# A hybrid decoder step: its last stage in scaled fp16 parts instead of fp32r parts, with weights split once

## The chip, the cores and the metric

The kernel runs on one core of a Trainium2 chip. The metric is the device time of one execution in microseconds (us). The core's engines run side by side: TensorE (PE in the profile; its weight loads are listed apart as PEld), VectorE (DVE), ScalarE (ACT), GpSimd (POOL), and SyncE (SP), which here issues nearly all DMAs, in its program's order. Every engine takes its own instructions in order and waits for the others by semaphores.

## The reference, cut to what matters

2048 prompt rows and 64 sample rows of width 1024 go through one mixer layer. All branches read the same normalised, conditioned `h`:

```python
proj = h @ w_in                                   # 1024 -> 10240
u_a, v_a, z_a, q, k, v, z_b, gate_logits = jnp.split(proj, SPLIT_IDX, axis=-1)
y_a = u_a * zs.reshape(bsz, s, A_WIDTH) * jax.nn.silu(z_a)      # zs: spatial gating of the normalised v_a
y_b = attn.reshape(bsz, s, B_OUT).astype(x.dtype) * jax.nn.silu(z_b)
g_a, g_b = jnp.split(jax.nn.sigmoid(gate_logits), 2, axis=-1)
merged = g_a * (y_a @ w_proj_a) + g_b * (y_b @ w_proj_b)        # 1024 -> 1024 and 512 -> 1024
out = merged @ w_out                                            # 1024 -> 1024
x_new = x + gate[:, None, :] * _rmsnorm(out, g_post)
```

All of it is float32 in the reference. The change touches the last four lines, and the place of some work that surrounds them.

## The kernel before

Each matrix product is done in parts: an operand is split into a high part H and a rest L, and three matmuls (H·H, L·H, H·L) add up in PSUM (`mm_cm`, lines 391 to 399, channels on partitions; `mm_tm`, lines 401 to 409, rows on partitions). For `w_in` the parts are fp16, scaled by a measured maximum (`parts`, lines 323 to 359: ACT takes the absolute maximum, then H on ACT at line 349 and L on DVE at line 350). In the last stage the parts are fp32r, without a scale.

The stages that matter here follow one another so:

1. Attention, with the q, k, v, z_b products and units 0 to 12 of the 16 gate units (`gates`, each 128 of the 2048 gate columns) woven in. Rows of `y_b` go to the DRAM tensor `yb_d` (`y_rows`, lines 1007 to 1013).
2. The four `v_a` units (lines 1118 to 1133), whose rows go to DRAM (`va_d`) and whose statistics are kept; then gate units 13 and 14 (lines 1134 to 1137).
3. Gating (lines 1192 to 1222): for each of 8 channel groups, `gating(g)` reads `va_d` back into tiles `vg`, ACT normalises them (line 1175), PE multiplies them with the spatial weights (line 1176) and DVE makes `zs` of that; the u and z units of the group follow in 5 column groups, with SiLU, and the product is written to `ya_d` (line 1213). `gating(g+1)` is woven into the matmuls of group g, but `gating(0)` stands alone ahead of them.
4. The first block of `y_a` is split (`y_split`, line 1247), under gate unit 15 (line 1248).
5. The last stage (lines 1262 to 1328): four blocks of rows, 512, 512, 512 and 576. Per block `y_a` and `y_b` are loaded and split, then for 8 groups of 128 channels PE makes the two projections (24 and 12 matmuls), DVE and ACT merge them with the gates and split the result (`mH`, `mL`, lines 1291 to 1295), and then the output product runs for 4 groups of 256 columns over the 4 or 5 row tiles of the block (line 1304, 24 matmuls each). `load_unit` (lines 293 to 305) loads and splits all three weights anew in every block. After the last column group of a row tile, the row tile of `x` is loaded into `xt`, the normalised product is added in place, and `xt` is written out (lines 1314 to 1328); `xt` has 3 buffers.

The order on each engine is set by a scheduler, which lists the instructions by times that it works out itself; `late` (lines 76 to 86) keeps one from being placed far ahead of its neighbours. Tiles of one tag take turns in a ring of `bufs` buffers, and a load into one waits for the last reader of the tile that was there. PSUM banks are rings too: three of tag `mm`, one each of `s0`, `s1` and `o`, two of `t` (line 100).

Of the kernel before, what the change touches and what calls it, by code (L numbers as in the profile page):

```python
# [69 lines left out]
def body(ctx, tc, I, O):  # L70
# [222 lines left out]
    def load_unit(w, c0, nc_=256, nkc=KC):  # L293

        out = []
        kt = 512 // nc_
        for j in range(0, nkc, kt):
            raw = wt.tile([128, kt, nc_], F32, tag="wr", bufs=6, name="wr")
            DMA(raw, w[j * 128:(j + kt) * 128, c0:c0 + nc_].rearrange("(k p) c -> p k c", p=128))
            H = wt.tile([128, kt, nc_], F32R, tag="wh", bufs=7, name="wh")  # L300
            L = wt.tile([128, kt, nc_], F32R, tag="wl", bufs=7, name="wl")
            S.activation(H, raw, AF.Copy)  # L302
            (nc.gpsimd if j == 4 else V).tensor_tensor(L, raw, H, op=ALU.subtract)  # L303
            out += [(H[:, k, :], L[:, k, :]) for k in range(kt)]
        return out

# [126 lines left out]
    def sample_attention(sp):  # L433
# [75 lines left out]
        for hp in range(4):  # L509
# [624 lines left out]
    for c in (13, 14):  # L1134
# [61 lines left out]
    for g in range(8):  # L1196
# [4 lines left out]
        for j, (t0, n) in enumerate(groups):  # L1201
# [32 lines left out]
    wt = fx.enter_context(tc.tile_pool(name="wt", bufs=1))
    f2 = None

    def y_split(pool, nm, src, k, c0, n):
        raw = (f2.tile([128, 576], F32, tag="raw", bufs=3, name="raw") if c0 else
               wt.tile([128, 512], F32, tag="wr", bufs=6, name="raw"))
# [117 lines left out]
```

## Time and profile before

| what | before |
|---|---|
| time, median of 3 runs | 2597.12 us (2596.55 to 2605.16) |
| time of the profiled execution | 2591.6 us |
| its span, first to last instruction | 2589.8 us |
| mean granted TensorE clock | 0.984 |
| PE busy | 2476.3 us, 96% of the span |
| DVE, ACT, POOL busy | 1610.8, 1123.6, 337.7 us |

The span is divided by time: attention and its products up to about 1640 us, the gating stage from 1706 to 2086 us, the last stage from 2110 to 2590 us. A matmul is pipelined, so its duration in the profile is longer than the time that it adds to a stream; that time is the distance between two starts, called the pitch here. Idle time of an engine that is not the bottleneck costs nothing.

### The profile page before, as it was taken

How to read it: one execution, taken by the hardware profiler on the slowest of the kernel's cores; microseconds unless marked ns; L12 is line 12 of the kernel's file. 1: busy time of each engine (PE TensorE's matmuls, PEld its weight loads, DVE VectorE, ACT ScalarE, POOL GpSimd, SP SyncE). 2: the span in 40 equal slices, each digit the busy share in tenths (PEclk: the TensorE clock that was granted, in tenths of full speed). 3: DMA queues.
4: the chain of work that ended last, by engine and by line, in shares of the span. 5: the costliest groups of instructions: out<-in, count | busy, mean ns of one | idle time of the engine just before them, and what ended most of it. 6: DMA issues, size and time to landing. Idle time of an engine off the chain costs nothing.

```text
span 2589.8 us, 48446 instructions
## 1 busy us (share of the span) xinstructions
PE 2476.3 (96%) x18518; PEld 1771.1 (68%) x18518; DVE 1610.8 (62%) x3630; ACT 1123.6 (43%) x2791; POOL 337.7 (13%) x458
## 2 busy tenths in 40 slices
PE   6899999989989999899899999999999999999998
PEld 3775867857668555555455688756565568898998
DVE  5743446788868788677796885665333245555653
ACT  5644565455545545444454432332232234343422
POOL 0210000220121211212113121011000011111110
PEclk7999999999999999999999999999999999999999
DMA  6323644666875777857768774352212066656552
GB/s 247 111 77 67 171 110 116 141 172 164 195 170 125 172 162 184 168 128 172 160 171 206 184 208 151 94 177 85 72 59 63 26 208 212 203 169 216 187 161 73
DMA packets 529992, 384.22 MB, mean 148 GB/s; under 512 B 185087, under 2 KB 472975, under 8 KB 529758
## 3 DMA queue, kind: packets, MB, share of 16 engines
q1 hardware_dynamic: 505150, 315.48, 45.1%
q0 software_dynamic: 24608, 65.63, 9.4%
q8 instruction: 145, 2.38, 0.4%
q14 instruction: 89, 0.73, 0.1%
HBM read 250.85 MB, written 90.78 MB: 132 GB/s over the span
## 4 chain that ended last, share of the span: by engine, by line
PE 58%; DMA 13%; DVE 12%; issue 11%; ACT 3%; POOL 1%; SPq 0%; DVEq 0%; ACTq 0%; POOLq 0%
PE mm L397 12%; PE mm L398 12%; PE mm L399 12%; DMA ch<-in_cache_kv_w 5%; PE mm L407 3%; PE mm L408 3%; PE mm L409 3%; DVE S L527 2%; DVE pr L526 1%; PE s L407 1%; PE s L1176 1%; PE s L409 1%; PE s L408 1%; PE o L409 1%; PE o L408 1%
## 5 line engine op out<-in xcount | busy, mean ns | idle before, releaser
L397 PE MATMUL mm<-hH,hl 128*128 128x512 f16 (+2 forms) x2240 | 767.6, 343 | 0.4 <-DVE xsm L428 0.4
L398 PE MATMUL mm<-hL,hl 128*128 128x512 f16 (+2 forms) x2240 | 767.0, 342 | 0.0
L399 PE MATMUL mm<-hH,hl 128*128 128x512 f16 (+2 forms) x2240 | 766.9, 342 | 0.0
L407 PE MATMUL mm<-hl,hH 128*128 128x256 f16 x1536 | 416.9, 275 | 13.7 <-ACT vt L676 10.9
L408 PE MATMUL mm<-hl,hL 128*128 128x256 f16 x1536 | 420.0, 275 | 3.7 <-DVE hL L668 3.4
L409 PE MATMUL mm<-hl,hH 128*128 128x256 f16 x1536 | 419.7, 274 | 0.5 <-DVE hl L350 0.5
L397 PEld LDWEIGHTS <-hl 128*128 128x128 f16 x2240 | 222.3, 99 | 182.9 <-issue 9.6
L399 PEld LDWEIGHTS <-hl 128*128 128x128 f16 x2240 | 219.6, 98 | 180.1 <-DVE hl L350 0.4
L398 PEld LDWEIGHTS <-hl 128*128 128x128 f16 x2240 | 219.9, 98 | 170.3 <-issue 1.0
L925 ACT ACTIVATE p<-p,sg 128x256 f32<-128x256 f32 (+1 forms) x384 | 172.4, 450 | 160.0 <-DVE sg L923 144.3
L454 POOL DMA_DIRECT2D ch<-in_cache_kv_w x104 | 93.1, 896 | 719.4 <-DVE pr L588 203.5
L408 PEld LDWEIGHTS <-hL 128*128 128x128 f16 x1536 | 151.3, 99 | 37.4 <-issue 13.6
L407 PEld LDWEIGHTS <-hH 128*128 128x128 f16 x1536 | 151.9, 99 | 28.0 <-issue 6.9
L409 PEld LDWEIGHTS <-hH 128*128 128x128 f16 x1536 | 151.5, 99 | 18.6 <-issue 0.4
L303 POOL TENSOR_TENSOR wl<-wr,wh 128x512 fp32r<-128x512 f32 x48 | 63.4, 1321 | 693.2 <-ACT wh L302 638.4
L302 ACT ACTIVATE wh<-wr 128x512 fp32r<-128x512 f32 x160 | 100.3, 631 | 120.3 <-PE mm L398 69.6
L923 DVE CUSTOM_DVE_ANT_0 p<-s,masks,cqk 128x256 f32<-128x256 f32 (+1 forms) x384 | 140.8, 419 | 14.6 <-PE s L915 14.3
L349 ACT ACTIVATE hl<-wr,scw 128x512 f16<-128x512 f32 x160 | 107.3, 713 | 82.0 <-DVE scw L341 77.3
L1209 ACT ACTIVATE e<-mm,scw 128x512 f32<-128x512 f32 (+2 forms) x40 | 24.5, 613 | 261.3 <-PE mm L399 261.3
L943 DVE SCALAR_TENSOR_TENSOR hl<-p,hl 128x1024 f16<-128x1024 f32 (+2 forms) x100 | 95.3, 954 | 51.3 <-ACT hl L942 50.8
L350 DVE SCALAR_TENSOR_TENSOR hl<-wr,scw,hl 128x512 f16<-128x512 f32 x160 | 114.9, 745 | 15.8 <-ACT hl L349 15.6
L397 PE MATMUL mm<-yaH,wh 128*128 128x512 f32 (+1 forms) x320 | 112.9, 353 | 0.5 <-DVE gts L1291 0.5
(441 smaller groups left out, 4619.2 us busy)
## 6 DMA issues: line engine op xcount, KB each, us to landing
ch<-in_cache_kv_w POOLq DMA_DIRECT2D x104, 512.0 KB, 6.0
wr<-in_w_in SPq DMA_DIRECT2D x160, 256.0 KB
wr<-in_w_proj_a SPq DMA_DIRECT2D x64, 256.0 KB
wr<-in_w_out SPq DMA_DIRECT2D x64, 256.0 KB
a<-sg SPq DMA_DIRECT2D x48, 264.0 KB
c<-a SPq DMA_DIRECT2D x48, 264.0 KB
v<-vt SPq DMA_DIRECT2D x96, 128.0 KB
vr<-v SPq DMA_DIRECT2D x48, 256.0 KB
```

The lines of the kernel that those rows point to most:

```text
L302: S.activation(H, raw, AF.Copy)
L349: S.activation(HL[:, 0], raw, AF.Copy, scale=sc[:, 0:1])
L350: V.scalar_tensor_tensor(HL[:, 1], raw, sc[:, 0:1], HL[:, 0], op0=ALU.mult, op1=ALU.subtract)
L397: PE.matmul(pt, h, xh[:, t0:t0 + n], start=kc == 0, stop=False)
L398: PE.matmul(pt, h, xl[:, t0:t0 + n], start=False, stop=False)
L399: PE.matmul(pt, l, xh[:, t0:t0 + n], start=False, stop=kc == m - 1)
L407: PE.matmul(pt, xh[:, t0:t0 + n], h, start=kc == 0, stop=False)
L408: PE.matmul(pt, xl[:, t0:t0 + n], h, start=False, stop=False)
L409: PE.matmul(pt, xh[:, t0:t0 + n], l, start=False, stop=kc == m - 1)
L923: V.tensor_tensor_reduce(x, sb[e][:, j, 0:nk], masks[:, 256 - nk:256], scale=cqk[:, i:i + 1], scalar=3e38, op0=ALU.add, op1=ALU.min, accum ...
L925: S.activation(x, x, AF.Exp, bias=mc, scale=-1.0, accum_out=lc)
L943: V.scalar_tensor_tensor(ll, x2, PSCALE, hh, op0=ALU.mult, op1=ALU.subtract)
```

## The change

- In the last stage both operands of all three products become scaled fp16 parts (`split`). Each scale is one over a global maximum: of each weight matrix (`wmx`, 40 tiles, scanned by 40 extra DMAs and 40 reductions on DVE during gating, `scan_weights`), and of `y_a` and `y_b` (`ymx`, one reduction for each piece written). The five maxima are brought together ahead of the last stage by a short chain over DVE, PE and DVE again (tiles `um`, `m1`, `fm`).
- The weights are loaded and split once (`weights16`) and stay on chip for all four blocks; the POOL's share of the splitting is gone. `w_proj_a`, the first block of `y_a` and `w_proj_b` are split under the last two gate units, `w_out` during the first block.
- Gate unit 14 is moved from between the `v_a` units and gating to the end of gating, next to unit 15.
- The merge takes one more ACT instruction per group (a scaled copy), the output product takes its PSUM banks from `s0`, `o`, `s1`, `t` in turn, and `xt` has 2 buffers instead of 3. The loads of `y_a` and `y_b` take a ring of 6 buffers (`raw`) which the weights share.

```diff
@@ plan
-        order.extend((OG + c * 128, 128) for c in (13, 14))
+        order.append((OG + 13 * 128, 128))
         for g in range(8):
             order.extend((o + g * 128, 128) for o in (OU, OZ))
-        order.append((OG + 15 * 128, 128))
+        order.extend((OG + c * 128, 128) for c in (14, 15))
@@ y_rows (and the same for the sample rows)
         S.activation(yT, pt, AF.Copy)
+        V.tensor_reduce(ymx[:, 40 + 5 * hp + q:41 + 5 * hp + q], yT, axis=AX.X, op=ALU.max, apply_absolute_value=True)
         DMA(yb_d[hp * 128:(hp + 1) * 128, q * 512:(q + 1) * 512], yT)
@@ after the v_a units
-    for c in (13, 14):
+    for c in (13,):
@@ gating stage
+    def scan_weights():
+        prev = None
+        for i, src in enumerate(tail_tiles()):
+            raw = wp.tile([128, 512], F32, tag="wr", bufs=WRB, name="wsc")
+            DMA(raw, src)
+            if prev is not None:
+                late(V.tensor_reduce(wmx[:, i - 1:i], prev, axis=AX.X, op=ALU.max, apply_absolute_value=True))
+            prev = raw
+            yield
...
             DMA(ya_d[g * 128:(g + 1) * 128, t0:t0 + n], zs[:, t0:t0 + n])
+            V.tensor_reduce(ymx[:, 5 * g + j:5 * g + j + 1], zs[:, t0:t0 + n], axis=AX.X, op=ALU.max,
+                            apply_absolute_value=True)
+            next(scan)
@@ between gating and the last stage
+    def split(pool, tag, raw, n, s, width=512):
+        H = pool.tile([128, width], F16, tag=tag + "H", bufs=1, name=tag + "H")
+        L = pool.tile([128, width], F16, tag=tag + "L", bufs=1, name=tag + "L")
+        S.activation(H[:, 0:n], raw[:, 0:n], AF.Copy, scale=s)
+        V.scalar_tensor_tensor(L[:, 0:n], raw[:, 0:n], s, H[:, 0:n], op0=ALU.mult, op1=ALU.subtract)
+        return H, L
+    um = f0.tile([128, 2, 5], F32, name="um")
+    for i, (x, lo, hi) in enumerate(((wmx, 0, 16), (wmx, 16, 24), (wmx, 24, 40), (ymx, 0, 40), (ymx, 40, 64))):
+        V.tensor_reduce(um[:, 0, i:i + 1], x[:, lo:hi], axis=AX.X, op=ALU.max)
+    pt = bank("t")
+    PE.transpose(pt[0:5, 0:128], um[:, 0, :], ident)
...
+    PE.matmul(pb[:, 0:5], ones[0:5, :], m1[:, 0:5], start=True, stop=True)
...
+    def weights16(pool, nm, w, nkc, s):
+        out = []
+        for k in range(nkc):
+            hl = []
+            for h in range(2):
+                raw = f0.tile([128, 576], F32, tag="raw", bufs=6, name="raw")
+                DMA(raw[:, 0:512], w[k * 128:(k + 1) * 128, h * 512:(h + 1) * 512])
+                hl.append(split(pool, f"{nm}{k}{h}", raw, 512, s))
+                yield
+            out.append(hl)
+        parts16[nm] = out
...
+    def first_block():
+        yield from weights16(f0, "wa", w_a, 8, um[:, 1, 0:1])
+        for k in range(8):
+            ya0.append(y_split(f0, "ya", ya_d, k, 0, 512, um[:, 1, 3:4]))
+            yield
+        yield from weights16(f0, "wb", w_b, 4, um[:, 1, 1:2])
-    ya0 = [y_split(f0, "ya", ya_d, k, 0, 512) for k in range(8)]
-    for _ in gates(15):
+    fb = first_block()
+    for c in (14, 15):
+        for _ in gates(c):
+            next(splitting)
+            for _ in range(3):
+                next(fb, None)
+    for _ in fb:
         pass
@@ last stage
-                    if k not in units:
-                        units[k] = [load_unit(w_a, k * 128, 128, 8), load_unit(w_b, k * 128, 128, 4)]
...
-                H = f1.tile([128, 576], F32R, tag=f"mH{c}", name=f"mH{c}")
+                H = f1.tile([128, 576], F16, tag=f"mH{c}", name=f"mH{c}")
...
+                    mm_cm(pa[:, 0:gn], unit_of("wa", c * 128, 128), ya, t0, gn)
...
+                    S.activation(ga, ga, AF.Copy, scale=fm[:, 0:1])
...
-                uo = load_unit(w_o, u * 256, 256, 8)
+                uo = unit_of("wo", u * 256, 256)
...
-                    po = bank(("s", "o")[i % 2])
+                    po = bank("sost"[i % 4])
...
-                    xt = f2.tile([128, D], F32, tag="xt", bufs=CXB, name="xt")
+                    xt = f2.tile([128, D], F32, tag="xt", bufs=2, name="xt")
```

The scheduler makes a new order of all this. Three places of it matter for what follows; rows of the changed kernel carry its own line numbers.

First, ScalarE at the start of gating, where `gt` is the eviction of a gate unit, `vg` the normalising of `gating(0)` and `hl` a weight split. Before:

```order
L720 ACTIVATE gt<-mm,scw 128x320
L349 ACTIVATE hl<-wr,scw 128x512 x2
L720 ACTIVATE gt<-mm,scw 128x512 x2
L1175 ACTIVATE vg<-vg,nb,rs 128x128 x2
L720 ACTIVATE gt<-mm,scw 128x512
L1175 ACTIVATE vg<-vg,nb,rs 128x128 x2
```

With the change:

```order
L711 ACTIVATE gt<-mm,scw 128x512 x2
L711 ACTIVATE gt<-mm,scw 128x256
L1167 ACTIVATE vg<-vg,nb,rs 128x128 x6
L711 ACTIVATE gt<-mm,scw 128x320
L1167 ACTIVATE vg<-vg,nb,rs 128x128
L339 ACTIVATE hl<-wr,scw 128x512
```

Before, the first `vg` stands behind all of unit 13 and two pieces of unit 14; now six `vg` stand ahead of the last piece of unit 13, and on PE the first matmul on `vg` follows 6 matmuls after unit 13.

Second, VectorE and PE at the end of gating, where the maxima come together (`um` the maxima by partition, `m` and `fm` what follows from them). VectorE with the change:

```order
L1224 SCALAR_TENSOR_TENSOR zs<-e,scw,zs 128x256
L1227 TENSOR_REDUCE ymx<-zs 128x1
L1217 SCALAR_TENSOR_TENSOR zs<-mm,scw,zs 128x320
L1223 SCALAR_TENSOR_TENSOR e<-e,mm 128x320
L1224 SCALAR_TENSOR_TENSOR zs<-e,scw,zs 128x320
L1227 TENSOR_REDUCE ymx<-zs 128x1
L1263 TENSOR_REDUCE um<-wmx 128x1 x3
L1263 TENSOR_REDUCE um<-ymx 128x1 x2
L1267 TENSOR_REDUCE m_24528<-t 5x1
L1268 TENSOR_SCALAR m_24528<-ident,m_24528 5x5
L1271 TENSOR_SCALAR um<-t 128x5
L1272 RECIPROCAL um<-um 128x5
```

and PE in the middle of gate unit 14:

```order
L388 MATMUL mm<-hL_112,hl 128x512
L1265 MATMUL t<-ident,um 5x128
L389 LDWEIGHTS hl
...
L389 MATMUL mm<-hH_109,hl 128x512
L1270 MATMUL t<-m_24528,ones 128x5
L387 LDWEIGHTS hl
```

The transpose of the maxima (line 1265) stands behind 38 matmuls of width 512 of unit 14, and the matmul that spreads them (line 1270) behind 22 more; no split of a weight can start earlier.

Third, SP at the very end. Before:

```order
L1328 DMA out<-xt 128x512 x2
L1316 DMA xt<-in_x_prompt 128x1024
L1328 DMA out<-xt 128x512 x4
L1316 DMA xt<-in_x_sample 64x1024
L1328 DMA out<-xt 128x512 x2
L1326 DMA out<-xt 64x512 x2
```

With the change:

```order
L1392 DMA out<-xt 128x512 x2
L1380 DMA xt<-in_x_prompt 128x1024
L1392 DMA out<-xt 128x512 x3
L1380 DMA xt<-in_x_prompt 128x1024
L1392 DMA out<-xt 128x512
L1380 DMA xt<-in_x_sample 64x1024
L1392 DMA out<-xt 128x512 x2
L1390 DMA out<-xt 64x512 x2
```

With two buffers three of the five loads of `xt` stand between writes, where two did.

More of the change, by code (lines that the diff above doesn't have):

```diff
@@ L161, in body @@
     vmx = const.tile([128, 3, 4, 16], F32, name="vmx")
+    wmx = const.tile([128, 40], F32, name="wmx")
+    ymx = const.tile([128, 64], F32, name="ymx")
+    V.memset(ymx, 0.0)
     w_cond = I["w_cond"][0]
+    w_a, w_b, w_o = I["w_proj_a"][0], I["w_proj_b"][0], I["w_out"][0]
     def x_src(i):
@@ L291, in gate_rows @@
             DMA(gg_d[:, n * 512:(n + 1) * 512], gr[:, 0, :])
[L293 to L305, printed above, removed]
     order, units, raws = [], {}, []
@@ L1190, in gating, with tail_tiles @@
         yield
+    def tail_tiles():
+        for w, n in ((w_a, 8), (w_b, 4), (w_o, 8)):
+            for k in range(n):
+                for h in range(2):
+                    yield w[k * 128:(k + 1) * 128, h * 512:(h + 1) * 512]
+    def scan_weights():
[7 more added lines that the diff above has]
+            yield
+        late(V.tensor_reduce(wmx[:, 39:40], prev, axis=AX.X, op=ALU.max, apply_absolute_value=True))
+        while True:
+            yield
+    scan = scan_weights()
     gen = gating(0)
@@ L1229, in body @@
     sx_.close()
+    next(scan)
     fx = ExitStack()
     f0 = fx.enter_context(tc.tile_pool(name="f0", bufs=1))
[L1234 to L1239, printed above, removed]
-        DMA(raw[:, 0:n], src[k * 128:(k + 1) * 128, c0:c0 + n])
-        H = pool.tile([128, 576], F32R, tag=f"{nm}H{k}", name=f"{nm}H{k}")
-        L = pool.tile([128, 576], F32R, tag=f"{nm}L{k}", name=f"{nm}L{k}")
-        S.activation(H[:, 0:n], raw[:, 0:n], AF.Copy)
-        V.tensor_tensor(L[:, 0:n], raw[:, 0:n], H[:, 0:n], op=ALU.subtract)
-        return H, L
@@ new lines, in body @@
+    pb = bank("t")
+    PE.matmul(pb[:, 0:5], ones[0:5, :], m1[:, 0:5], start=True, stop=True)
+    V.tensor_scalar(um[:, 0], pb[:, 0:5], 1.0 / 8192.0, 1e-30, op0=ALU.mult, op1=ALU.max)
+    V.reciprocal(um[:, 1], um[:, 0])
+    fm = f0.tile([128, 6], F32, name="fm")
+    for i in range(2):
+        V.tensor_tensor(fm[:, i:i + 1], um[:, 0, i:i + 1], um[:, 0, 3 + i:4 + i], op=ALU.mult)
+    V.scalar_tensor_tensor(fm[:, 2:3], fm[:, 1:2], 0.5, fm[:, 0:1], op0=ALU.mult, op1=ALU.add)
+    V.tensor_scalar(fm[:, 2:3], fm[:, 2:3], 2.0 ** 37 / 2.0 ** 15, 1e-30, op0=ALU.mult, op1=ALU.max)
@@ new lines, in unit_of, with y_split @@
+    def unit_of(nm, c0, nc_):
+        h, o = divmod(c0, 512)
+        return [(x[h][0][:, o:o + nc_], x[h][1][:, o:o + nc_]) for x in parts16[nm]]
+    parts16 = {}
+    def y_split(pool, nm, src, k, c0, n, s):
+        raw = f0.tile([128, 576], F32, tag="raw", bufs=6, name="raw")
+        DMA(raw[:, 0:n], src[k * 128:(k + 1) * 128, c0:c0 + n])
+        return split(pool, f"{nm}{k}", raw, n, s, 576)
+    def first_block():
+        yield from weights16(f0, "wa", w_a, 8, um[:, 1, 0:1])
+        for k in range(8):
+            ya0.append(y_split(f0, "ya", ya_d, k, 0, 512, um[:, 1, 3:4]))
+            yield
+        yield from weights16(f0, "wb", w_b, 4, um[:, 1, 1:2])
@@ L1263, in body @@
             mg = []
[L1264 to L1282 removed]
+            ya = [y_split(f0, "ya", ya_d, k, c0, n, um[:, 1, 3:4]) for k in range(8)] if c0 else ya0
+            yb = [y_split(f2, "yb", yb_d, k, c0, n, um[:, 1, 4:5]) for k in range(4)]
+            for c in range(8):
+                H = f1.tile([128, 576], F16, tag=f"mH{c}", name=f"mH{c}")
+                L = f1.tile([128, 576], F16, tag=f"mL{c}", name=f"mL{c}")
                 gt = f2.tile([128, 2, 576], F32, tag="gts", bufs=2, name="gts")
@@ L1296, in body @@
                 mg.append((H, L))
+                for _ in range(2):
+                    next(wo, None)
+            for _ in wo:
+                pass
             tl = [(t, min(128, n - t)) for t in range(0, n, 128)]
```

39 lines of the change are left out of this document (17 added, 22 removed).

## The prediction

> **What bounds the kernel now.** I read the page first, then the busy times by stretch of time, then the list of waits of PE in the last stage.
>
> ```profile
> span 2589.8 us, 48446 instructions
> PE 2476.3 (96%) x18518; PEld 1771.1 (68%) x18518; DVE 1610.8 (62%) x3630; ACT 1123.6 (43%) x2791; POOL 337.7 (13%) x458
> ```
>
> ```profile
> 1200.00:1400.00 200.00, 178.89 (x1365) 105.69 (x1363) 149.71 (x327) 91.61 (x240) 34.50 (x51) 0.96 0.73 174
> 1706.00:2086.00 380.00, 379.22 (x2234) 224.06 (x2233) 150.20 (x293) 108.93 (x250) 17.28 (x27) 1.00 0.22 70
> 2110.00:2582.00 472.00, 466.93 (x3073) 429.28 (x3072) 245.54 (x440) 177.42 (x390) 61.62 (x47) 1.00 0.57 182
> ```
>
> After the stretch each row gives PE, PEld, DVE, ACT and POOL busy, the granted clock, the DMA share and GB/s. Gating (second row) and the last stage (third) are PE's: it is idle for 0.8 and 5.1 us of them, at full clock. DVE has room there (150 of 380, 246 of 472 us), DMA too. In attention (first row) PE is idle for 21 of 200 us while DVE is busy for 150.
>
> ```profile
> PE s L407 <- DVE ot L1310: 3.6, 3, 1.6
> PE mm L397 <- DVE gts L1291: 0.5, 1, 0.5
> PE s L407 <- ACT mH L1294: 0.5, 1, 0.5
> ```
>
> So the splitting and reloading of weights in the last stage costs the end nothing now: PE waits for none of it. Removing 160 ACT splits, 160 DVE or POOL subtractions and some 20 MB of loads (two passes over 10.5 MB of weights instead of four) is worth nothing by itself. What can be won there is the pitch of PE's matmuls; what can be lost is cover at the seams.
>
> **Term 1, the pitch.** These are starts of matmuls in PE's order of time, the first and the last of a run without a gap: fp32r with `y_a` (24 matmuls), `y_b` (9), width 288 (17) and the output product (24); then fp16 of width 512, 256 and 320 (24 each).
>
> ```profile
> 2152.24 0.39 PE L397 MATMUL mm<-yaH,wh 128*128 128x512 f32 x1
> 2157.47 0.39 PE L399 MATMUL mm<-yaH,wl 128*128 128x512 f32 x1
> 2150.13 0.40 PE L397 MATMUL mm<-ybH,wh 128*128 128x512 f32 x1
> 2152.00 0.40 PE L399 MATMUL mm<-ybH,wl 128*128 128x512 f32 x1
> 2446.80 0.29 PE L399 MATMUL mm<-yaH,wl 128*128 128x288 f32 x1
> 2448.91 0.29 PE L397 MATMUL mm<-yaH,wh 128*128 128x288 f32 x1
> 2420.94 0.28 PE L407 MATMUL o<-wh,mH 128*128 128x256 f32 x1
> 2423.62 0.28 PE L409 MATMUL o<-wl,mH 128*128 128x256 f32 x1
> ```
>
> ```profile
> 1726.29 0.38 PE L398 MATMUL mm<-hL,hl 128*128 128x512 f16 x1
> 1731.26 0.38 PE L397 MATMUL mm<-hH,hl 128*128 128x512 f16 x1
> 1701.78 0.27 PE L397 MATMUL mm<-hH,hl 128*128 128x256 f16 x1
> 1704.29 0.27 PE L399 MATMUL mm<-hH,hl 128*128 128x256 f16 x1
> 1704.55 0.30 PE L397 MATMUL mm<-hH,hl 128*128 128x320 f16 x1
> 1707.67 0.30 PE L399 MATMUL mm<-hH,hl 128*128 128x320 f16 x1
> ```
>
> fp32r: 5.23/23 = 0.2274 us with `y_a`, 1.87/8 = 0.2338 with `y_b`, 2.11/16 = 0.1319 at 288, 2.68/23 = 0.1165 at 256. fp16: 4.97/23 = 0.2161 at 512, 2.51/23 = 0.1091 at 256, 3.12/23 = 0.1357 at 320. Width 288 in fp16 stands in no row; halfway between 256 and 320 it is 0.1224. The counts are from the code: three blocks of 512 give 3·8·24 = 576 matmuls with `y_a` and 288 with `y_b`; the fourth block runs 2·8·36 = 576 of width 288; the output product 4·17·24 = 1632 of width 256. So 576·0.0113 = 6.5, 288·0.0177 = 5.1, 576·0.0095 = 5.5, 1632·0.0074 = 12.1: **−29.2 us**. With the 288s at the pitch of 320 or of 256 it would be −21.5 or −36.9; the three fp16 rows lie on a line, so I keep −29.2 within 1.
>
> The Trainium skill, "TensorE: Matmul & The Clock Gate", section "Back-to-back issue gap", gives the warm gap as N/2.4 ns plus 2.5 ns and names no type. By that alone both kinds would run at 0.2158, 0.1225 and 0.1092 us and this term would be zero. The trace agrees with it for fp16 and not for fp32r, so the rows decide.
>
> **Term 2, `gating(0)` loses half of its cover.**
>
> ```profile
> 1664.75 0.38 ACT L427 ACTIVATE xsm<-mm 64x256 f32<-64x256 f32 x1 [0.66 <-PE mm L417]
> 1686.54 1.48 SPq L1169 DMA_DIRECT2D vg<-va  x3
> 1689.85 6.25 DMA vg<-va
> 2171.49 2.88 DMA raw<-ya
> 1710.51 0.49 PE L1176 MATMUL s<-wT,vg 128*128 128x128 f32 x2 [0.78 <-ACT vg L1175]
> 1710.77 5.49 ACT L1175 ACTIVATE vg<-vg,nb,rs 128x128 f32<-128x128 f32 x14
> ```
>
> The first row is the end of the `v_a` units on PE (1664.7), and the two gate units behind it end at about 1707.8, so one takes 21.5 us. The loads of `vg` are issued from 1686.5, held back by the statistics and the `lr` tiles, not by PE, and the small last one lands at 1696.1. Before, unit 14 covered that; PE waited 0.8 us. Now PE has unit 13 only, to 1686.2, and 6 matmuls (1.3 us): it asks for `vg` at 1687.5. The first quarter can land between 2.9 us after its issue (a read of `ya_d` of the same size, the third row from below) and 6.25 us: 1689.4 to 1692.8; one normalising later PE has stood for 2.3 to 5.7 us. From there 16 normalisings at 0.39 us (5.49/14) take as long as the 16 small and some 20 wide matmuls between them, but an eviction and a split (0.5 and 0.7 us) stand in ACT's line. **+5 us**, bounds +2 and +9.
>
> **Term 3, the start of the last stage.** Unit 14 now helps here: two units, 43 us, cover the maxima and 32 tiles, then the first projection (24·0.2161 = 5.2 us) covers 4 tiles of `y_b`.
>
> ```profile
> 2088.74 0.53 ACT L1209 ACTIVATE e<-mm,scw 128x320 f32<-128x320 f32 x1 [6.05 <-PE mm L399]
> 2089.82 0.55 DVE L1211 SCALAR_TENSOR_TENSOR zs<-e,scw,zs 128x320 f32<-128x320 f32 x1
> 2110.00:2130.00 20.00, 19.49 (x85) 15.66 (x85) 8.47 (x13) 7.03 (x13) 3.57 (x3) 1.00 0.87 270
> 2185.68 0.69 DVE ybL L1244
> ```
>
> ```profile
> L349 ACT ACTIVATE hl<-wr,scw 128x512 f16<-128x512 f32 x160 | 107.3, 713 | 82.0 <-DVE scw L341 77.3
> L350 DVE SCALAR_TENSOR_TENSOR hl<-wr,scw,hl 128x512 f16<-128x512 f32 x160 | 114.9, 745 | 15.8 <-ACT hl L349 15.6
> ```
>
> Let T be the end of the last z matmul (2088.5 in this trace). The last `zs` is done at T+1.9, its maximum and the five small ones at about T+3. But PE's order puts the transpose behind 38 matmuls, T+8.2, and the spreading behind 60, T+13.0; with the small DVE steps the first split starts at about T+14. The six tiles of the ring have landed by then, and DVE takes them at 0.745 us each: T+19. From there each tile needs its load. At the 270 GB/s of the third row 262 KB take 0.97 us. Until the first tile of `y_b` that is 27 tiles, and about 1.2 MB of gate results to write, worth 4.7 more: 31.7·0.97 = 31 us, T+50. PE asks at T+42.8+5.2 = T+48, and the other three `y_b` tiles come 0.97 us apart against 0.65 us of matmuls each: **+3 us**. ACT needs 24·0.713+4 us of gate evictions for the tiles of the first projection, so it is not the bound. If a tile took as long as at a block's seam (from that read at 2171.49 to the last row of the first fence: 12 tiles with a ring of 3 in 14.9 us, 1.24 each, or 1.65 if three had been loaded before), it would be +11 to +23; if DVE alone set the pace, 0.745, nothing. Bounds 0 and +12.
>
> **Term 4, the end.** `xt` has two buffers.
>
> ```profile
> 2570.89 0.42 DVE L1310 SCALAR_TENSOR_TENSOR ot<-s,ggp 128x256 f32<-128x256 f32 x1 [2.39 <-ACT sq L1309]
> 2575.72 0.34 SPq L1316 DMA_DIRECT2D xt<-in_x_prompt  x1
> 2576.62 4.57 DMA out<-xt
> 2581.21 3.83 DMA xt<-in_x_sample
> ```
>
> The chain that ends last is not PE there, but the ring: a write of 4.57 us, a load of 3.83. Call the first row (row tile 0 of the last columns) E. The load that waits for tile 0's write is issued at E+4.8 (second row), the sample rows land at E+14.2, and the span ends at E+18.9. With two buffers tile 2 loads at E+4.8 and lands near E+8.7; tile 3 waits for tile 1's write, loads near E+10 and lands near E+13.8; the sample tile waits for tile 2's write, loads at E+12.6 to E+15 and lands at E+16.4 to E+18.8. The end moves by +2.2 to +4.6 against E, and 0.7 us of term 1 (96 matmuls behind E) no longer counts: **+4 us**, bounds +2 and +6.
>
> The Trainium skill, "DMA: Bandwidth & Descriptors", section "Anatomy of one DMA — SWDGE (gpsimd) path", gives 2.0 us plus bytes at 436 GB/s for one transfer on that path. Taken over to SP's it would be an estimate of 2.6 us for a write here where the trace has 4.57, the sample tile would land at about E+14.7, and this term would be +1.
>
> **Term 5, waits in the last stage.** The 3.6 us for `ot` (quoted) arise at block seams, when DVE splits the next block first. The same tiles stand ahead there still, though the ring is deeper and more banks take turns. Taken: −1 us, bounds −4 and +3. The extra scaled copy on ACT (40 of them, ACT 177 of 472 us busy, 160 splits gone) lies under the `y_b` matmuls; without that cover it would cost 0.7 us a group.
>
> **Term 6, reductions on DVE.**
>
> ```profile
> L527 DVE TENSOR_REDUCE S<-pr 128x8 f32<-128x512 f32 x64 | 43.5, 680 | 0.8
> ```
>
> A maximum over 512 columns is nearest to this row, 0.68 us. 40 of them for the weights and up to 40 for `y_a` (some 50 us) go into gating's 230 us of idle DVE, behind three PSUM banks of 5.2 us: nothing. The 40 scan loads meet a DMA share of 0.22 there: nothing. Of the 16 for `y_b` about 12 fall into attention, 8.2 us of DVE; all of it on the path would be +8. PE is idle there for only a tenth of the time, so most lies beside: **+1 us**, bounds −3 (a luckier order) and +8.
>
> **Sum.** −29.2 + 5 + 3 + 4 − 1 + 1 = −17.2 us on the profiled execution (2591.6 → 2574.4). That execution lies 5.5 us below the median of the runs, 2597.1, so the median to expect is **2580 us**.
>
> **The rivals.** *Full gain* (14%): `vg` lands early and the ring keeps up, terms 2 and 3 near +2 and 0: 2597 − 25 or better, 2566 to 2572. For it: DMA moves over 270 GB/s in places; against: PE's order fixes T+13. *Gain mostly eaten* (17%): terms 2, 3 and 6 near their upper bounds, +9, +12, +4: 2596. For it: DVE leads PE's waits in attention, and the seam's 1.24 us a tile.
>
> *Slower* (5%): the ring refills one tile after another, because SP takes its DMAs in order, gate results among them, and a blocked write to `gt_d` holds all loads behind it. Each tile then costs a load, two splits and a restart. From 1.65 us a tile (30 tiles to the last of `y_b`, ready at T+69 against T+48) the sum is zero; at 2.2 us it is ready at T+85, 37 us late, and the time 2597 − 20 + 37 = 2614. Against it: six loads are in flight where the seam has three.
>
> *No faster matmuls* (3%): the pitch of the last stage is set by something other than the type, term 1 is zero, and the losses remain: 2609. Against it: the fp16 rows come from the same loops at the same clock.
>
> **How the numbers follow.** My forecast, 2571 to 2589, has 61%. The range takes the full gain and most of the eaten one: 2566 to 2595. About 0.5%, 13 us, is what a measurement of this kernel can tell from no change; the line is at 2584. Faster: 14% and five sixths of 61%, 0.65. Same: the rest of 61% and the eaten gain, 0.27. Slower: 0.08.
>
> **What would show it.** In the profile after: fp16 pitches of 0.216, 0.122 and 0.109 us in the last stage; PE standing for `vg` at the start of gating for 3 to 7 us; PE standing at the first `y_b` product, or for a bank, for 0 to 8 us; the chain of waits ending in two turns of `xt`; PE otherwise without waits from gating on. Wrong it would be if PE's idle time in attention moved by more than 5 us, if gating grew waits for `wr` tiles, or if the pitch stayed at 0.227.

## The result, and the profile after

| kernel | median of its runs | ratio to the kernel before, 95% interval |
|---|---|---|
| before, beside it | 2597.97 us (2596.55 to 2605.16) | 1 |
| changed | 2582.68 us (2578.64 to 2582.92) | 0.9932 (0.9911 to 0.9953) |
| changed, in a later set of 8 runs | 2582.92 us (2579.31 to 2587.12) | 0.9953 (0.9930 to 0.9975) |

The change is faster, by 0.5 to 0.7%, about as much as a measurement here can tell. The profiled execution has a span of 2581.1 us, against 2589.8 before.

The page of the changed kernel, its head and its first part:

```profile
span 2581.1 us, 47947 instructions
PE 2454.3 (95%) x18521; PEld 1646.5 (64%) x18521; DVE 1624.9 (63%) x3675; ACT 1088.9 (42%) x2711; POOL 274.3 (11%) x410
```

Busy times by stretch, changed kernel: a piece of attention, then from the last matmul of the `v_a` units to the last tanh of a z unit, then from the last gate unit to PE's last matmul (length; PE, PEld, DVE, ACT, POOL busy; granted clock, DMA share, GB/s):

```profile
1200.00:1400.00 200.00, 179.88 (x1363) 106.18 (x1362) 150.76 (x328) 92.46 (x241) 34.11 (x50) 0.95 0.70 174
1667.00:2081.40 414.40, 406.12 (x2368) 239.78 (x2365) 222.56 (x435) 121.41 (x275) 20.89 (x31) 0.99 0.34 105
2124.10:2564.30 440.20, 437.50 (x3077) 300.67 (x3075) 189.98 (x343) 129.84 (x291) 0.00 (x0) 1.00 0.34 110
```

The same two stretches of the kernel before:

```profile
1664.40:2088.70 424.30, 423.52 (x2487) 248.88 (x2486) 180.29 (x355) 124.50 (x279) 20.89 (x31) 1.00 0.26 81
2109.50:2581.20 471.70, 467.14 (x3076) 429.45 (x3075) 244.74 (x439) 177.50 (x389) 62.12 (x47) 1.00 0.57 182
```

The last stage is 31.5 us shorter. The stretch with gating should be shorter by the gate unit that left it, 21.5 us, and is shorter by 9.9 only: 11.6 us are lost there. PE, idle for 0.8 us of it before, is now idle for 8.3 us, and the granted clock is no longer full.

Four marks cut every run of this study into the same parts, in us of its profiled execution. "Ahead" is everything up to the last matmul of the `v_a` units; "gating" runs from there to the start of the last tanh; "gate units" to the last matmul of the gate units that stand at the end; "last stage" to PE's last matmul; "tail" to the end of the span.

| kernel | ahead | gating | gate units | last stage | tail | all but "ahead" |
|---|---|---|---|---|---|---|
| before | 1664.4 | 424.3 | 20.8 | 471.7 | 8.6 | 925.4 |
| changed | 1667.0 | 414.4 | 42.7 | 440.2 | 16.8 | 914.1 |
| e1, before again | 1677.1 | 424.8 | 20.8 | 473.0 | 8.4 | 927.0 |
| e2, three `xt` | 1665.9 | 413.7 | 42.8 | 437.5 | 10.9 | 904.9 |
| e3, unit 14 back | 1655.6 | 424.5 | 21.4 | 461.8 | 14.1 | 921.8 |
| e4, no weight scan | 1664.0 | 415.8 | 42.7 | 439.1 | 13.4 | 911.0 |
| e5, fp16 alone | 1662.5 | 425.0 | 20.8 | 448.0 | 8.7 | 902.5 |
| e6, unit 12 moved, three `xt` | 1658.7 | 431.4 | 42.8 | 438.8 | 11.1 | 924.1 |
| e7, filled stand | 1673.3 | 416.8 | 42.7 | 440.4 | 15.5 | 915.4 |
| e8, `vg` first, three `xt` | 1663.6 | 409.4 | 42.8 | 437.8 | 9.7 | 899.7 |
| e9, and `sel` 2 steps later | 1663.9 | 406.3 | 42.7 | 438.5 | 11.1 | 898.6 |
| e10, changed again | 1667.0 | 414.3 | 42.8 | 439.2 | 16.9 | 913.2 |
| e11, and `sel` 5 steps later | 1664.0 | 402.9 | 42.8 | 438.3 | 11.2 | 895.2 |

The column "ahead" moves by 12.7 us between two executions of the kernel before, while the other parts of those two agree within 1.6 us in all. So the parts behind it tell effects of a few us that a single time does not.

**The pitch.** Starts of matmuls in the last stage of the changed kernel, the first and the last of a run without a gap: 24 with `y_a`, 12 with `y_b`, 24 of width 288, 21 of the output product:

```profile
2180.01 0.38 PE L387 MATMUL mm<-ya0H,wa01H 128*128 128x512 f16 x1
2184.97 0.38 PE L389 MATMUL mm<-ya7H,wa71L 128*128 128x512 f16 x1
2235.72 0.38 PE L387 MATMUL mm<-yb0H,wb00H 128*128 128x512 f16 x1
2238.10 0.38 PE L389 MATMUL mm<-yb3H,wb30L 128*128 128x512 f16 x1
2471.53 0.29 PE L387 MATMUL mm<-ya0H,wa00H 128*128 128x288 f16 x1
2474.34 0.29 PE L389 MATMUL mm<-ya7H,wa70L 128*128 128x288 f16 x1
2397.73 0.27 PE L397 MATMUL s<-wo00H,mH 128*128 128x256 f16 x1
2399.91 0.27 PE L399 MATMUL s<-wo60L,mH 128*128 128x256 f16 x1
```

4.96/23 = 0.2157 us, 2.38/11 = 0.2164, 2.81/23 = 0.1222 and 2.18/20 = 0.1090: the forecast's 0.2161, 0.1224 and 0.1091, the interpolated one too.

**The loss in gating.** PE's waits between the end of the `v_a` units and the last tanh, changed kernel (total, times, longest):

```profile
PE t L592 <- DVE acc L583: 3.8, 1, 3.8
PE s L1168 <- DMA vg<-va: 2.8, 1, 2.8
PE t L329 <- DVE mx L327: 1.3, 1, 1.3
PE s L1168 <- issue: 0.4, 1, 0.4
```

The forecast had the second row. The first is a product of the sample attention, which still runs in this stage: one piece of PE work with `acc`, which DVE has not finished. The third is a wait for the maximum of a weight unit; it is DVE that stands there first, 1.90 us at 1738.3 for a load of cache rows, also of the sample attention. Behind the two long stands something else happens. The first stand and the stretch behind it, then the stretch at the second, which ended at 1772.4:

```profile
1690.20:1693.00 2.80, 0.02 (x1) 0.00 (x0) 0.00 (x0) 0.52 (x2) 0.00 (x0) 1.00 0.86 248
1693.66:1697.07 3.41, 3.41 (x14) 2.68 (x13) 1.07 (x3) 3.41 (x10) 0.00 (x0) 0.50 0.75 217
...
1772.17:1775.58 3.41, 3.15 (x15) 3.15 (x16) 2.80 (x5) 0.00 (x0) 0.00 (x0) 0.50 0.16 63
```

The granted clock (the figure before the DMA share) is 0.50 for 3.41 us at each stand, from about its end on, and full again behind that. PE counts as busy there, and works at half speed: two matmuls of width 512 that follow each other are then 0.42 us apart, not 0.216.

```profile
1695.60 0.63 PE L387 MATMUL mm<-hH,hl 128*128 128x512 f16 x1
1696.02 0.64 PE L388 MATMUL mm<-hL,hl 128*128 128x512 f16 x1
```

Waits of 8.3 us less 0.8 before, and 2 x 3.41 x 0.50 = 3.4 us of lost clock, are 10.9 of the 11.6. The Trainium skill, "TensorE: Matmul & The Clock Gate", section "What's actually happening", says that the clock falls to half after an idle window of 3413 ns that runs freely, and rises again after a busy one. The trace agrees on the half (0.50) and on the length of the slow stretch (3.41 us), but a stand of 2.80 us, shorter than that window, was enough.

**The start of the last stage.** ACT's first split of a weight and its splits of `y_b`, and the matmul that asks for the latter, changed kernel (T, the end of the last z matmul, is 2081.4 here):

```profile
2095.18 0.72 ACT L1256 ACTIVATE wa00H<-raw,um 128x512 f16<-128x512 f32 x1 [2.63 <-DVE um L1272]
2126.46 0.71 ACT L1256 ACTIVATE yb0H<-raw,um 128x512 f16<-128x512 f32 x1
2127.21 0.75 DVE L1257 SCALAR_TENSOR_TENSOR yb0L<-raw,um,yb0H 128x512 f16<-128x512 f32 x1 [0.58 <-ACT yb0H L1256]
2129.80 0.38 PE L387 MATMUL mm<-yb0H,wb00H 128*128 128x512 f16 x1
```

The first split starts at T+13.8, `y_b` is ready at T+46.6, and PE asks for it at T+48.4. PE does not wait there.

**The tail.** Out of the chain that ended last, changed kernel:

```profile
2557.21 4.56 DMA out<-xt
2561.84 4.04 DMA xt<-in_x_prompt
...
2567.99 4.50 DMA out<-xt
2572.56 3.80 DMA xt<-in_x_sample
```

Two full turns of the ring, write and load, stand behind one another: 16.8 us from PE's last matmul to the end, against 8.6.

### The profile page after: what moved, and what is told of

The parts are those of the page before. It is cut to its first block, busy times and chain, and to the rows that moved or that the text cites. A ratio compares the mean times of both kernels' runs of the same rounds, so it can differ in the third digit from the quotient of the medians.

```text
span 2581.1 us, 47947 instructions
## 1 busy us (share of the span) xinstructions
PE 2454.3 (95%) x18521; PEld 1646.5 (64%) x18521; DVE 1624.9 (63%) x3675; ACT 1088.9 (42%) x2711; POOL 274.3 (11%) x410
## 3 DMA queue, kind: packets, MB, share of 16 engines
q8 instruction: 145, 2.38, 0.4%
## 4 chain that ended last, share of the span: by engine, by line
PE 51%; issue 17%; DMA 14%; DVE 12%; ACT 3%; POOL 1%; SPq 0%; DVEq 0%; ACTq 0%; POOLq 0%
PE mm L387 11%; PE mm L388 10%; PE mm L389 10%; DMA ch<-in_cache_kv_w 6%; PE mm L397 3%; PE mm L398 3%; PE mm L399 3%; DVE S L517 2%; DVE pr L516 2%; PE s L397 1%; PE s L399 1%; DMA wc<-in_w_cond 1%; PE s L398 1%; DVE p L914 1%; PE s L1168 1%
## 5 line engine op out<-in xcount | busy, mean ns | idle before, releaser
L324 ACT ACTIVATE junk<-wr 128x512 f16<-128x512 f32 x160 | 99.2, 620 | 0.3
L667 ACT ACTIVATE vt<-mm,scw 128x256 f32<-128x256 f32 x96 | 44.3, 469 | 116.5 <-PE mm L399 59.4
L479 POOL DMA_DIRECT2D q<-qs x96 | 50.4, 532 | 391.4 <-DVE pr L516 311.8
```

What stands on the lines that cost most here:

```text
L324: late(S.activation(junk, raws[j].rearrange("p k c -> p (k c)"), AF.Abs, accum_out=mx[:, j:j + 1]))
```

## The experiments

**e1: the kernel before, unchanged,** to learn how far two executions agree.

> The kernel before, unchanged, with a second profile. The medians say that the change is worth 15.3 us, the two profiled executions 8.7 us (2591.6 and 2582.9). If the first profile of before was a fortunate execution, this one has a span near 2595 and the missing 5 us show in a stage ahead of gating (attention), since gating and the last stage are PE's without a wait. If profiled executions of before are always faster than timed ones, the span is near 2590 again and the time near 2597.

2594.47 us, ratio 1.0011 (0.9987 to 1.0036). The profiled execution is 14.3 us longer than the other one, and 12.7 of that lie ahead of gating. The same wait in the two, of the kernel before and of e1, over everything ahead of the end of the `v_a` units:

```profile
PE mm L407 <- ACT vt L676: 10.9, 4, 5.6
```

```profile
PE mm L407 <- ACT vt L676: 18.2, 3, 14.8
```

So what happens in attention differs by chance by more than most terms of the forecast.

**e2: three buffers for `xt`.**

```diff
-                    xt = f2.tile([128, D], F32, tag="xt", bufs=2, name="xt")
+                    xt = f2.tile([128, D], F32, tag="xt", bufs=3, name="xt")
```

> The changed kernel with three buffers for xt again, nothing else. Theory: the end, 16.6 us from PE's last matmul to the end of the span against 8.4 before, is the ring of two turns of write (4.5 to 5.3 us) and load (3.8 to 4.0 us) more than PE's work: with three buffers it is near 8.5 us again and the time falls by 8 us, to about 2574.5. Rival: the loads are slow there for another reason (the order of SP's queue), and only the 4 us of my prediction, or nothing, comes back: 2578 to 2583.

2571.53 us (2567.59 to 2575.35), ratio 0.9916 (0.9888 to 0.9944). The chain has one turn of the ring left:

```profile
2558.25 4.54 DMA out<-xt
2562.81 3.23 DMA xt<-in_x_sample
```

The tail is 10.9 us, 5.9 less than in the changed kernel. That lies between the two expectations: one turn of the ring is gone, but 2.3 us more than in the kernel before are left. Over the study the runs of the changed kernel with two buffers have tails of 13.4 to 16.9 us, those with three 9.7 to 11.2. The intervals of the two ratios overlap, so the size of the gain is the trace's, not the runs'.

**e3: unit 14 back ahead of gating.**

```diff
-        order.append((OG + 13 * 128, 128))
+        order.extend((OG + c * 128, 128) for c in (13, 14))
...
-        order.extend((OG + c * 128, 128) for c in (14, 15))
+        order.append((OG + 15 * 128, 128))
...
-    for c in (13,):
+    for c in (13, 14):
...
-    for c in (14, 15):
+    for c in (15,):
```

> The changed kernel with gate unit 14 back between the v_a units and gating, so that only unit 15 covers the splits at the start of the last stage. Theory A: all of the 12 us lost in gating (2.8 us for vg, 3.8 us for the sample attention's acc, 1.3 us for a maximum, and a halved clock behind the two long waits) is missing cover, so PE's waits in gating fall under 1.5 us and gating takes 11 to 12 us less beside the 21.5 us of the unit; the last stage then stands 15 to 24 us for its splits, with a halved clock behind that: 2590 to 2598 in all. Theory B: the acc wait comes from the 80 added reductions on DVE; it stays, and the time is 4 to 6 us higher than that.

2593.39 us, ratio 0.9992 (0.9971 to 1.0013): as fast as the kernel before. Gating is 424.5 us again, with one wait in it (first row), and the last stage has the stands that the two units had covered (the other rows, PE's waits from the last tanh to the end):

```profile
PE s L1168 <- ACT vg L1167: 1.0, 1, 1.0
...
PE mm L387 <- ACT yb0H L1256: 10.1, 1, 10.1
PE mm L387 <- ACT ya0H L1256: 8.3, 1, 8.3
```

So the place of unit 14 makes the loss in gating, with everything else of the change left in, and it is worth its price: moving it costs 11.6 us there and saves 21.6 here (461.8 against 440.2).

**e4: no scan of the weights.** The 40 loads and 40 reductions of the scan are left out, and the maxima of the weights are a constant, 0.25; the scales are then not the measured ones.

```diff
+    V.memset(wmx, 0.25)
...
-            next(scan)
...
-    next(scan)
```

> The changed kernel without the scan of the weights: no scan loads, no reductions of them, the three weight maxima are the constant 0.25. Theory A (the position of unit 14): gating keeps its waits, the time changes by less than 2 us. Theory B (DVE's added reductions make acc late): the 3.8 us wait for acc and the clock lost behind it go, 5 to 7 us less, about 2576.

2580.52 us, ratio 0.9941 (0.9921 to 0.9961). Gating takes 415.8 us, and the two waits are there:

```profile
PE t L593 <- DVE acc L584: 5.2, 1, 5.2
PE s L1169 <- DMA vg<-va: 2.7, 1, 2.7
```

The scan costs nothing that can be seen, and its work on DVE is not why `acc` is late.

**e5: the type alone.** The kernel before with fp16 parts in the last stage, by constant scales; the weights are loaded and split in every block as before, units 13 and 14 stand ahead of gating, and no maximum is taken, so that it fits these inputs only.

```diff
-            H = wt.tile([128, kt, nc_], F32R, tag="wh", bufs=7, name="wh")
-            L = wt.tile([128, kt, nc_], F32R, tag="wl", bufs=7, name="wl")
-            S.activation(H, raw, AF.Copy)
-            (nc.gpsimd if j == 4 else V).tensor_tensor(L, raw, H, op=ALU.subtract)
+            H = wt.tile([128, kt, nc_], F16, tag="wh", bufs=7, name="wh")
+            L = wt.tile([128, kt, nc_], F16, tag="wl", bufs=7, name="wl")
+            S.activation(H, raw, AF.Copy, scale=2.0 ** 16)
+            V.scalar_tensor_tensor(L, raw, 2.0 ** 16, H, op0=ALU.mult, op1=ALU.subtract)
```

(and so for `y_a` and `y_b` with 8, for the merged product with 2^-15, and 2^-21 in place of 0.5 at the end).

> The kernel before with one thing changed: the last stage's operands are fp16 parts at constant powers of two (2^16 for the weights, 8 for y, 2^-15 for the merged product) in place of fp32r parts. It leaves out the maxima and the scales computed from them, so it fits these inputs only. Weights are still loaded and split in every block, units 13 and 14 stand ahead of gating and 15 at the end, as before. My theory (term 1 is the type of the matmul's operands): the pitches become 0.216, 0.122 and 0.109 us, the last stage is shorter by 28 to 31 us than in the kernel before, gating is unchanged, and the time is 2565 to 2569 where the kernel before has about 2596. Rival (the last stage of the changed kernel became shorter because weights are no longer loaded and split again): no more than 5 us are gained, 2591 or more.

2564.64 us (2562.79 to 2573.5), ratio 0.9876 (0.9852 to 0.9900). The last stage by stretch, and PE's waits in it:

```profile
2108.30:2556.30 448.00, 440.00 (x3076) 301.20 (x3074) 264.03 (x486) 173.56 (x389) 0.00 (x0) 1.00 0.61 192
```

```profile
PE s L407 <- DVE ot L1310: 5.0, 3, 2.1
PE mm L397 <- DVE gts L1291: 2.3, 2, 1.3
```

PE's busy time falls from 467.1 to 440.0 us with the same number of matmuls, so the type of the operands makes the gain, and splitting each weight four times costs PE little. The stage is 23.7 us shorter, not the 28 to 31 expected: DVE has taken over POOL's subtractions (264 us against 245), PE's idle time rises from 4.6 to 8.0, and behind one of its stands, of 2.1 us, the clock is at 0.50 for 3.4 us, which costs 1.7 more. Of the 32 us between the medians the trace shows 22.9 behind the `v_a` units; the rest lies ahead, where chance moves as much.

**e6: unit 12 out of attention,** so that two units stand ahead of gating and two at its end; three buffers for `xt`.

```diff
-        ...11: (10, 11, 12)}.get(i, ())
+        ...11: (10, 11)}.get(i, ())
...
-    for c in (13,):
+    for c in (12, 13):
```

> The changed kernel with three buffers for xt and gate unit 12 taken out of attention: units 12 and 13 now stand ahead of gating, 14 and 15 ahead of the last stage. Theory of cover: from the end of the v_a units to the last tanh there are 402.8 + 21.5 = 424.3 us again, PE waits under 1.5 us there; the end keeps the 8 us that three buffers gave; attention gives up 21.5 us if unit 12 was work like any other there, and less if it filled PE's idle time. So the time is 2571.5 - 11.6 = 2560 if attention gives all of it back, and 2571 if it gives back half. Rival (gating's loss comes from what is new beside it, not from the missing unit): the loss of 11 us stays and the time is 2571 or more with attention giving all back.

2582.03 us, ratio 0.9931 (0.9906 to 0.9956): 22 us above the best case expected and 11 above the other, and the theory of cover holds for `vg` alone. Gating is 431.4 us and not 424.3. The wait for `vg` is gone, as the cover would have it, but this one stands there:

```profile
PE t L592 <- DVE acc L583: 5.2, 1, 5.2
```

And what lies ahead of gating gives back only 7.2 us of the 21.5 against e2 (1658.7 against 1665.9), a figure that chance alone can move by more (12.7 us between e1 and the kernel before). The end of attention, in e2 and then in e6:

```profile
1400.00:1600.00 200.00, 195.36 (x1652) 146.88 (x1651) 161.19 (x373) 83.53 (x208) 41.29 (x68) 1.00 0.68 192
```

```profile
1400.00:1600.00 200.00, 186.59 (x1602) 144.50 (x1601) 155.62 (x369) 80.34 (x210) 38.12 (x63) 0.97 0.67 182
```

PE is idle for 13.4 us there where it was for 4.6, as it would be if unit 12 had filled time in which PE waits. And the wait for `acc` does not hang on what stands next to gating, but on how many gate units stand ahead of it in all: with 15 (before, e3, e5) it is not there, with 14 (changed, e2, e4, e6, e7) it is. In the code each piece of a gate unit takes the sample attention one step further, and each column group of gating three; why DVE is late with 14 is argued from that (about 4.3 us a step under a unit, 3.5 in gating), and not shown. DVE's own stands do not explain it: on the way to the product it stands for loads of `vg` and of cache rows for 12.9 and 8.7 us in the changed kernel (7.0 and 6.1 before), but only for 5.9 and 4.3 us in e8 below, where `acc` comes as late.

**e7: the stand for `vg` filled** with 13 matmuls whose result nobody reads.

```diff
+    pf = bank("mm")
+    for i in range(13):
+        PE.matmul(pf, hT[0][0][:, 0:128], hT[0][0][:, 0:512], start=i == 0, stop=i == 12)
     for _ in gen:
         pass
```

> The changed kernel with 13 idle matmuls of width 512 (their result is read by nobody) ahead of gating's first product, 2.8 us of work in place of the 2.8 us in which PE stands for vg. Theory (a stand of PE is followed by some 3.4 us at half the granted clock, and costs half of that on top of itself): the granted clock in the 3.5 us after the first product is 0.95 or more where it was 0.54, the pitch there 0.22 us in place of 0.43, and the stretch from the end of the v_a units to the last tanh shortens by 1 to 2 us from 414.4. Rival (gating's start is slow there for its own work, small products between wide ones and ACT's normalising): the pitch stays at 0.43 us and nothing is gained.

The clock after the first product, and from the end of the later stand for `acc` on:

```profile
1699.10:1702.60 3.50, 3.13 (x16) 2.20 (x16) 0.26 (x1) 3.50 (x10) 0.00 (x0) 1.00 0.73 215
1778.86:1785.69 6.83, 5.82 (x25) 5.28 (x26) 5.14 (x10) 0.00 (x0) 1.75 (x3) 0.50 0.22 82
```

The clock stays full where PE was kept at work, so the slow stretch follows from the stand and not from gating's own work. Time was not gained: gating takes 416.8 us, 2.4 more than without the filling. PE waits 1.1 us for `vg` and 1.7 us for the normalising, and the slow clock at the other stand lasts for 6.83 us in place of 3.41. The one time of this kernel, 2590.5 us, has 6.3 us more ahead of gating, and says nothing.

**e8: the loads of `vg` first.** The first `gating(0)` puts its loads on SP's queue ahead of the statistics and the `lr` tiles, which get a ring of their own; three buffers for `xt`.

```diff
+    gen = gating(0)
+    zs = next(gen)
     V.memset(mv, 0.0)
...
-        lr = vp.tile([128, 17, 128], F32, tag="vg", bufs=2, name="lr")[0:64, 0:6, :].rearrange(
+        lr = vp.tile([128, 6, 128], F32, tag="lr", bufs=2, name="lr")[0:64, 0:6, :].rearrange(
...
-    gen = gating(0)
-    zs = next(gen)
```

> The changed kernel with three buffers for xt, and the loads of vg for the first gating put on SP's queue ahead of the statistics and the lr tiles, which get buffers of their own. Theory (PE stands 2.9 us for vg because the loads are issued behind the lr tiles, and the clock that falls after it costs about as much again as half of 3.4 us): the wait for vg goes, the granted clock after gating's first product stays at 0.95 or more, and from the end of the v_a units to the last tanh there are 408 to 410 us in place of 413.7; the time is 2565 to 2568 where the kernel with three buffers alone had 2571.5. Rival (vg was not what came last: the statistics or ACT's normalising come late as well): PE waits as long for ACT, the stretch stays at 412 us or more, and the time at 2570 or more.

2568.33 us, ratio 0.9902 (0.9879 to 0.9926), gating 409.4 us. The only wait left in it, and the clock after gating's first product:

```profile
PE t L592 <- DVE acc L583: 4.6, 1, 4.6
```

```profile
1685.30:1688.80 3.50, 3.50 (x25) 2.43 (x24) 2.91 (x8) 2.92 (x7) 0.00 (x0) 1.00 0.41 124
```

The first load of `vg` is issued at 1611.4 us here and at 1689.3 in the changed kernel. So the wait for `vg` came from what its loads stood behind: the `lr` tiles, in SP's order and in the ring of buffers that the two shared. Both were changed at once, and which of them held the loads was not tried. 4.3 us are gained in gating against e2, with a longer wait for `acc` in it.

**e9: and the products with `sel` of the last sample unit two steps later.** These are the products for which PE waits for `acc`.

```diff
-            for _ in range(4):
+            for _ in range(4 if hp < 3 else 6):
                 yield
             pa = bank("t")
```

> As the run before it, and the products with sel of the last sample unit come two steps later in PE's order (about 7 us). Theory (the wait for acc, 2.8 to 5.2 us, is a product that stands too early in PE's order since one gate unit fewer lies ahead of gating): the wait for acc goes with the clock that falls behind it, the stretch from the end of the v_a units to the last tanh is 403 to 406 us, against 402.8 for no loss at all, and the time is 2560 to 2564, which beats both kernels. Rival (DVE is behind by then and the products behind it wait as long): the stretch stays at 408 us or more and the time at 2565 or more.

2566.79 us, ratio 0.9904 (0.9876 to 0.9932), gating 406.3 us; the wait for `acc` is 2.8 us instead of 4.6. The stretch lies between the two expectations, the time on the side of the rival. Without the later products the wait is 2.8 (e2) to 5.2 us (e4, e6), so this run shows no effect of two steps, and the times cannot tell it from e8.

**e10 and e11: the changed kernel again, and five steps in place of two,** on one chip.

```diff
-            for _ in range(4 if hp < 3 else 6):
+            for _ in range(4 if hp < 3 else 9):
```

> The changed kernel unchanged, beside the next kernel on one chip, so that the two can be compared without the differences between chips. Expected: a ratio to the kernel before of 0.991 to 0.996; from the end of the v_a units to the last tanh 413 to 416 us, with the waits for vg and acc; from PE's last matmul to the end of the span 13 to 17 us.

> Three buffers for xt, the loads of vg ahead of the lr tiles, and the products with sel of the last sample unit five steps later (about 17 us) in place of two. Theory (they stood too early in PE's order): no wait for acc is left, and from the end of the v_a units to the last tanh there are 402.5 to 404.5 us, against 406.3 with two steps. Against the changed kernel on this chip 12 to 20 us are gained: 11 to 12 between those two points, 5 at the end, the rest by chance ahead of them. Rival (DVE is behind for another reason): the wait stays 2 us or more, and the stretch at 406 us.

| kernel | median | ratio to the kernel before, 95% interval |
|---|---|---|
| e10, the changed kernel | 2582.92 us (2579.31 to 2587.12) | 0.9953 (0.9930 to 0.9975) |
| e11 | 2563.55 us (2555.84 to 2569.39) | 0.9879 (0.9856 to 0.9901) |

PE's waits in gating in e10, and the slow stretch behind its stand for `vg`; then the same waits in e11, and the whole of gating in e11 by stretch:

```profile
PE t L592 <- DVE acc L583: 3.8, 1, 3.8
PE s L1168 <- ACT vg L1167: 2.5, 1, 2.5
PE t L329 <- DVE mx L327: 2.0, 1, 2.0
```

```profile
1693.68:1697.09 3.41, 3.41 (x14) 2.69 (x13) 1.35 (x3) 3.41 (x9) 0.00 (x0) 0.50 0.78 226
```

```profile
PE mm L387 <- DVE zs L1217: 0.8, 1, 0.8
```

```profile
1660.00:2070.00 410.00, 409.21 (x2418) 242.08 (x2417) 226.22 (x443) 123.42 (x279) 20.89 (x31) 1.00 0.33 102
```

The waits and the slow clock are gone, so five steps are enough and the product had stood too early in PE's order; gating takes 402.9 us, where the kernel before less one gate unit gives 424.3 - 21.5 = 402.8. The kernel e11 is faster than both others: its interval lies below that of the changed kernel on the same chip, the medians are 19.4 us apart, and the trace shows 18.0 of them behind the `v_a` units (913.2 against 895.2).

## Why the prediction was right, and where its terms were not

The forecast was 2580 us with a range of 2566 to 2595; the runs gave 2582.7, and the case that was held likeliest (a gain by the pitch, part of it given back at the seams) is what happened. On the profiled execution, from the end of the `v_a` units on, the terms of the sum make -18.2 us and the trace shows -11.3. So the closeness of 2582.7 to 2580 is in part luck: the sum was 6.9 us too favourable where it can be checked, and terms 2 and 4 came out above their own bounds. Term by term:

| term | forecast | shown | by |
|---|---|---|---|
| 1, pitch | -29.2 | -29.6 | PE busy in the last stage, 467.1 to 437.5; e5 |
| 2, cover of `gating(0)` | +5 (+2 to +9) | +11.6 | gating less one unit; e3 takes it back, e11 too |
| 3, start of the last stage | +3 (0 to +12) | 0 | no wait for `y_b`; with one unit of cover, e3, +21.6 |
| 4, ring of `xt` | +4 (+2 to +6) | +8.2; +4.8 to +8.3 in all runs with two buffers | tail; e2 |
| 5, waits in the last stage | -1 (-4 to +3) | -1.9 | PE idle, 4.6 to 2.7 |
| 6, reductions on DVE | +1 (-3 to +8) | not to be told from chance | "ahead", +2.6, against 12.7 between two runs of one kernel |

The moved unit is 21.5 us shorter in gating and 21.9 longer at its end; these 0.4 us are in no term.

**Term 1** was right in size and cause: the pitches came out within 0.001 us, and e5 has most of the gain, 27.1 us of PE busy time, with nothing else of the change. "No faster matmuls" falls with it. So does the reading that saved loads and splits would gain by themselves, which the forecast had priced at nothing.

**Term 2 was mis-sized, and is where most of the miss comes from.** The step that failed is to take the stand for `vg` ("PE has stood for 2.3 to 5.7 us"), and ACT's line behind it, as the whole of the loss. The stand for `vg` is 2.8 us, inside these bounds. Two more things were not foreseen, so the forecast's "PE otherwise without waits from gating on" did not come true. One is that a unit ahead of gating also takes the sample attention forward: with one fewer, its last product with `acc` stands too early in PE's order for DVE, 3.8 us, and this is 80 us further on; 1.3 us more are the wait for a weight unit's maximum, behind DVE's stand for cache rows. The forecast looked for what waits next to the moved unit, and not for work that is paced by PE's matmuls and so moves with them. The other is the clock: the sum counted a stand as idle time alone, while 3.41 us at half the clock come with each of the two long ones, 1.7 us more. That the stand for `vg` goes when its loads are issued earlier is shown by e8.

**Term 3** was too high by 3 us. Its first step, T+14, was exact (T+13.8), and `y_b` was there 1.8 us ahead of PE's question, where the forecast had it 2 us behind. The step that failed is the ring: the forecast gave DVE five us for the six tiles that had landed, and 31 us of loads after that; in the trace the 32 tiles ahead of `y_b`, those six among them, take 31.3 us together (2095.18 to 2126.46), 0.98 each.

**Term 4** was too low by 4 us. The mechanism is the one described (two turns of `xt` end the chain). The size failed at the writes: the forecast let the first free its buffer 3.0 us after its issue, as in the kernel before, and the later one after 2.5 to 4.9. In the changed kernel's chain they take 4.56 and 4.50 us by themselves. The Trainium skill's price of a transfer, quoted there from "DMA: Bandwidth & Descriptors", section "Anatomy of one DMA — SWDGE (gpsimd) path", made an estimate of 2.6 us for such a write and would have been further off.

**Terms 5 and 6** are small, and the second cannot be told. The check named in the forecast, PE's idle time in attention, is 65.8 us against 66.6 from 200 us to 24.4 us ahead of the end of the `v_a` units, so it did not move.

**The rivals.** "Mostly eaten" was near in what it said of gating, but wanted losses at the start of the last stage and in attention that are not there. The slower one, a ring that refills one tile after another, did not come: the ring of six kept a tile per 0.98 us, where that rival needed 1.65. But there were only 1.8 us to spare between `y_b` and PE, and with one unit less of cover (e3) the whole gain is gone.

## What to carry to other kernels

Work that one engine does between two stages is cover twice: for the loads beside it, and for every piece of work that is paced by its steps, so when it is moved, look at both, as far down the program as that pacing reaches. Where PE would stand for about 2 us or more, count the stand, and as a risk half of 3.4 us or more of slow clock with it. Before a gain is paid for with cover, ask whether the wait is one of order, or of a shared buffer, alone: here the loads put first, one product a few steps later and one more buffer gave back 18 us without touching the matmuls.

## What the hardware showed that was not expected

- **The clock can fall after a short stand of PE, and need not.** Stands of 2.49 (e10), 2.80 and 3.81 us (changed kernel) came with 3.41 us at a granted clock of 0.50, and a wide fp16 matmul then takes 0.42 us in place of 0.216. In e2 a stand of 1.87 us that ended at 1738.75 was enough (first row), and one of 2.77 us that ended at 1772.19 was not (second row); one of 2.04 us in e10 was not either. After the 1.1 us that were left in e7 it stayed at 1.00. In e7 the stand for `acc`, 3.80 us, came with 6.83 us at 0.50, where the changed kernel's, 3.81 us, had 3.41. What decides between these is open; no threshold follows from the runs.

```profile
1739.50:1742.91 3.41, 3.41 (x15) 1.98 (x13) 3.41 (x6) 0.00 (x0) 0.88 (x1) 0.50 0.17 46
...
1772.19:1775.60 3.41, 3.40 (x27) 2.98 (x28) 3.38 (x8) 0.00 (x0) 1.11 (x2) 1.00 0.09 35
```

- **fp32r matmuls have a longer pitch than fp16 ones at full clock,** by 5 to 8% at each width met here: 0.2274 and 0.2157 us at 512, 0.1319 and 0.1222 at 288, 0.1165 and 0.1090 at 256. With `y_b` the fp32r pitch was 0.2338 and the fp16 one 0.2164; why the two operands differ in fp32r was not tried. The weight loads of the last stage (PEld) became shorter as well, from 429.5 to 300.7 us for 3075 of them; whether they or the matmuls themselves set the longer pitch was not tried either.
